# Moving one residual step and one set of feature combinations of a hybrid encoder block, and laying the FFN's buffers over dead ones

## The chip, the cores and the metric

The kernel runs on one core of a Trainium2 chip. A core has five engines that run side by side, each through its own queue in order: TensorE (matmuls and transposes; PE in the profile, PEld for its weight loads), VectorE (DVE), ScalarE (ACT), GpSimd (POOL) and SyncE (SP), which here issues nearly all DMA transfers. The metric is the device time of one execution in microseconds, lower is better.

## The reference

One layer of a residual block on 2048 tokens of width 1024, everything in float32:

```
h   = rms_norm(x);  proj = h @ w_in
yA  = chunk_band_attention(q, k, v, rel_bias)      # 8 heads, band of 9 chunks of 64
yB  = rwkv7_time_mix(...)                          # recurrent state over time
m   = sigmoid(gA) * (yA @ proj_a) + sigmoid(gB) * (yB @ proj_b)
x   = x + rms_norm(m @ w_out)
u   = square(relu(rms_norm(x) @ w_up)) @ w_down    # 1024 -> 4096 -> 1024
x   = x + rms_norm(u)
```

## The kernel before

The 2048 tokens are cut into four groups of 512 (g = 0 to 3). Every float32 matmul operand is split into a rounded part and a remainder (`split`, lines 69 and 70: ScalarE casts the high part, VectorE subtracts it), and a product is made of three matmuls (`mm3`, line 78).

*Mixing.* For each group: the recurrent part, attention, then `phase_merge`. The merge first computes eight branches of A (`branch`, lines 927 to 932: load a gate block th from gd, load and split a block of proj_a, 12 matmuls into ps_p, then VectorE multiplies), adds the B branch mb that was stored to md (line 948), and splits the sum into mh and ml. Then it runs the w_out loop (line 958): two halves n of eight blocks k, each block 4 x 3 matmuls into ps_o. After each half ScalarE copies ps_o to o (line 964), and o is stored to od (line 1229).

*Work laid beside.* `after` is a generator of steps that the merge calls between its w_out blocks in the second half and empties at its end. In the first three groups it prepares the next group's features. From group 1 on it runs `residuals(g - 1)`: for each of four tiles of 128 tokens it loads o and x, normalises (ACT lines 980 and 987, POOL lines 94 to 99, VectorE lines 982 to 989), stores x1, transposes xn on TensorE (ps_ht, line 994, 8 transposes per tile) and stores the result to ht (line 997). In group 3 it first runs `combinations(0)`, which reads the stored features ht of groups 0 and 1 and writes four differences of feature blocks to td (lines 1018 to 1025). They are the operands of the FFN's up stage, which saves one of eight block products by Strassen's scheme (in Winograd's form).

*FFN.* Two halves of two groups each: `phase_up` and `phase_down`. `first_half` loads and splits bl and bh (lines 1031 to 1039), the features of the half's first group. `phase_up` makes in its first eight steps products that need only those (A11 B11, A12 B21), with the splits of the other operands T (t2, t3, t1, b22, t4, from td and ht, line 1069) between them; then come 16 steps with the rest. The hidden values go to DRAM (ad, line 1094). `phase_down` has 16 steps (fg) of 96 matmuls into ps_dn (line 78), whose results VectorE adds into u (lines 1170 and 1172); its operands fop are loaded and split one step at a time. After th = 1 of each step but the last it runs one step of `beside`: the residual of group 3 (four steps), `combinations(1)` (four), `first_half(2)` (four). In the last step `final` normalises, adds x1 and stores the result (lines 1178 to 1193).

*Order and memory.* The program's order is that of the Python calls as a priority; the tile framework places instructions of each engine, and may put later work ahead where it is ready. SBUF is handed out by pools as two stacks, one from the left and one from the right. When a pool closes, its bytes go to the next pool, and a tile there waits until the tiles that were in those bytes are done (`reuse_waits="tile"`). So the places of the pools settle what a load or a split must wait for.

Before the change, in the FFN the left stack has z (32 KB per partition), b (32 KB) and raw (16 KB), then in the up stage the weight operands ops (28 KB) and the T operands (80 KB), and in the down stage ring (32 KB) and ffo; the right stack has cb, then up or the sums u.

Of the kernel before, what the change touches and what calls it, by code (L numbers as in the profile page):

```python
# [49 lines left out]
class Block:  # L50
# [883 lines left out]

    def phase_merge(self, g, o, between):

        tc, nc, a = self.tc, self.nc, self.a
        with ExitStack() as ctx:
# [70 lines left out]
    def combinations(self, half, mp):  # L1009


        nc = self.nc
        KH = KB // 2
        g0, g1 = (self.ht[2 * half + i] for i in range(2))
        for k in range(KH):
            b = mp.tile([P, 4, G], F32, tag="cmb", bufs=1, name="cmb")
            for i, src in enumerate((g0[:, k], g1[:, k], g0[:, KH + k], g1[:, KH + k])):
                nc.sync.dma_start(b[:, i], src)
            t = mp.tile([P, 4, G], F32, tag="cmt", bufs=1, name="cmt")
            for o, x, y in (  # L1020
                (t[:, 0], b[:, 1], b[:, 0]), (t[:, 2], b[:, 3], b[:, 1]),
                (t[:, 1], b[:, 3], t[:, 0]), (t[:, 3], b[:, 2], t[:, 1]),
            ):
                nc.vector.tensor_tensor(o, x, y, ALU.subtract)
            nc.sync.dma_start(self.td[half][:, :, k], t)
            yield
# [7 lines left out]
    def first_half(self, g, bp):  # L1034

        bh, bl = (bp.tile([P, KB, G], F32R, tag="b" + x, name="b" + x) for x in "hl")
        for k in range(0, KB, 2):
# [3 lines left out]
            yield  # L1041
        self.b1 = bh, bl

    def phase_up(self, half, zp, rp, cb, pn, early):
# [6 lines left out]
        with ExitStack() as ctx:  # L1051
            e = ctx.enter_context
            sp = e(tc.tile_pool(name="ops", bufs=1, reuse_waits="tile"))
            tb = e(tc.tile_pool(name="ht", bufs=1, reuse_waits="tile"))
# [4 lines left out]
            T = {}  # L1059

            def operands():
                td, g1 = self.td[half], self.ht[2 * half + 1]
                for n, src in (
                    ("t2", td[:, 1]), ("t3", td[:, 2]), ("t1", td[:, 0]), ("b22", g1[:, hi4]), ("t4", td[:, 3])
                ):
                    h, l = T[n] = [tb.tile([P, KH, G], F32R, name=n + x) for x in "hl"]
                    for k in (0, 2):
# [69 lines left out]
    def phase_down(self, half, zp, rp, cb, pn, beside_of):  # L1137
# [4 lines left out]
        with ExitStack() as ctx:  # L1142
            e = ctx.enter_context
            ring = e(tc.tile_pool(name="ring", bufs=2, reuse_waits="tile"))
            op = e(tc.tile_pool(name="ffo", bufs=2, reuse_waits="tile"))
            pt = e(tc.tile_pool(name="ffp", bufs=2, space=PSUM, reuse_waits="tile"))
            cp = e(tc.tile_pool(name="ffu", bufs=1, side="right", reuse_waits="tile"))
            u = [cp.tile([P, D], F32, name=f"u{t}") for t in range(NT)]
            beside = beside_of(op, pt)

# [44 lines left out]
            for fg in range(NF // 2):  # L1195
                ws = [load(2 * fg), load(2 * fg + 1)]
                last = fg == NF // 2 - 1
                if last:
                    gt = self.gain(op, a["post_ffn_g"], "g_post2", 2)
                for th in range(2):  # L1200
                    down(th, ws, fg == 0)
                    if last:
                        final(th)
                    elif th:
                        advance(beside, 1)


    def run(self):
        tc, e = self.tc, None
        with ExitStack() as ctx, ExitStack() as mixing:  # L1210
# [10 lines left out]
            for g in range(self.NG):  # L1221
                self.phase_rwkv(g)
                self.phase_attention(g)
                with tc.tile_pool(name="p0", bufs=2, reuse_waits="tile") as sp, \
                     tc.tile_pool(name="p0p", bufs=2, space=PSUM, reuse_waits="tile") as pt:
                    o = [sp.tile([P, D], F32, tag="o", bufs=GT, name=f"o{t}") for t in range(GT)]
                    self.phase_merge(g, o, self.after(g, sp, pt))
                    for t in range(GT):
                        self.nc.sync.dma_start(self.od[g][t], o[t])
# [56 lines left out]
```

## Time and profile before

| | us |
|---|---|
| median of 3 runs | 3496.29 |
| lowest and highest of them | 3493.8, 3499.4 |
| the profiled execution | 3489.82 |
| span of its profile | 3488.1 |

In the profile, a row of the engines' summary gives busy time, its share of the span and the number of instructions. A row of the timeline gives the start, the length, the engine, the line of the kernel, the operation, the tile written and the tiles read, the shape and the count; in brackets stands how long the engine was idle before it, and what released it. A line such as L69 or L78 is that of a helper, so the tile's name tells which stage it is from. The stages follow one another in the span so: the four mixing groups up to 2113 us, the first up stage up to 2454, the first down stage up to 2807, the second up stage up to 3119, the second down stage up to the end.

### The profile page before, as it was taken

What the parts mean: (1) busy time and instruction counts of PE and PEld (TensorE: products, weight loads), DVE (VectorE), ACT (ScalarE), POOL (GpSimd) and SP (SyncE); (2) the same over time, 40 slices, a digit from 0 to 9 for tenths busy, and PEclk for the clock granted to TensorE, in tenths of its full rate; (3) what the DMA queues carried; (4) which work ended last, traced back from release to release, by engine and by line L of the source; (5) the groups of instructions that cost most, each with busy time, mean ns of one, the idle gap of its engine ahead of it and who ended that gap; (6) DMA issues with size and microseconds to landing.
All of it is one profiled execution on the core that took longest, in us unless ns stands there. A gap on an engine that the chain in (4) does not pass through costs nothing. (4 is left out here: it accounts for less than half of the span.)

```text
span 3488.1 us, 50851 instructions
## 1 busy us (share of the span) xinstructions
PE 3312.6 (95%) x19233; PEld 2679.4 (77%) x19233; DVE 2425.0 (70%) x4206; ACT 1430.4 (41%) x2399; POOL 353.4 (10%) x700
## 2 busy tenths in 40 slices
PE   7999999999998999999999986999999989999998
PEld 5777777777876777877777875888888878888886
DVE  5774756756756766856775865777876687776667
ACT  4434644436644436635445635333311143331112
POOL 2210002100012110002110000111100021100001
PEclk9999999999999999999999998999999999999999
DMA  5223453125364125365224279434753274343333
GB/s 148 79 86 124 137 180 116 60 91 179 128 224 148 59 86 183 111 226 163 65 92 143 88 243 301 134 121 137 246 190 97 87 241 140 109 156 97 97 97 109
DMA packets 430125, 481.15 MB, mean 138 GB/s; under 512 B 19564, under 2 KB 322864, under 8 KB 429880
## 3 DMA queue, kind: packets, MB, share of 16 engines
q1 hardware_dynamic: 419640, 444.34, 39.9%
q0 software_dynamic: 10240, 33.56, 2.5%
q8 instruction: 151, 2.47, 0.3%
q14 instruction: 94, 0.77, 0.1%
HBM read 356.16 MB, written 124.81 MB: 138 GB/s over the span
## 5 line engine op out<-in xcount | busy, mean ns | idle before, releaser
L78 PE MATMUL ps_dn<-fop 128*128 128x512 f32 x3072 | 698.3, 389 | 1.7 <-DVE u L1172 1.7
L78 PEld LDWEIGHTS ps_dn<-fop 128*128 128x128 f32 x3072 | 576.1, 188 | 122.0 <-DVE u L1172 2.6
L78 PE MATMUL psd<-hh,whi 128*128 128x512 f32 x1344 | 546.8, 407 | 17.1 <-ACT whi L69 14.0
L78 PE MATMUL psd<-hl,whi 128*128 128x512 f32 x1344 | 543.8, 405 | 0.0
L78 PE MATMUL psd<-hh,wlo 128*128 128x512 f32 x1344 | 540.6, 402 | 0.7 <-DVE wlo L70 0.5
L69 ACT CAST whi<-wraw 128x1024 fp32r<-128x1024 f32 (+1 forms) x296 | 255.7, 864 | 582.3 <-PE psd L78 391.6
L70 DVE TENSOR_TENSOR wlo<-wraw,whi 128x1024 fp32r<-128x1024 f32 (+1 forms) x296 | 292.6, 989 | 257.7 <-ACT whi L69 193.5
L1172 DVE TENSOR_TENSOR u<-u,ps_dn 128x512 f32<-128x512 f32 x480 | 323.5, 685 | 175.3 <-PE ps_dn L78 174.6
L78 PEld LDWEIGHTS psd<-hh,whi 128*128 128x128 f32 x1344 | 257.8, 192 | 71.5 <-ACT whi L69 15.7
L78 PEld LDWEIGHTS psd<-hh,wlo 128*128 128x128 f32 x1344 | 257.6, 192 | 52.8 <-DVE wlo L70 3.6
L78 PEld LDWEIGHTS psd<-hl,whi 128*128 128x128 f32 x1344 | 258.3, 192 | 48.5
L69 ACT CAST fop<-wdraw 128x1024 fp32r<-128x1024 f32 x64 | 67.3, 1051 | 469.8 <-DVE u L1172 321.5
L78 PE MATMUL ps_p<-yh,whi 128*128 128x512 f32 x256 | 107.3, 419 | 23.8 <-DVE th L932 23.4
L1094 POOL DMA_DIRECT2D ad<-r x128 | 69.6, 544 | 573.2 <-DVE r L1093 556.6
L69 ACT CAST s12h<-s 128x1024 fp32r<-128x1024 f32 x32 | 33.6, 1051 | 185.8 <-PE ps_u L78 185.8
L826 DVE CUSTOM_DVE_ANT_0 sc<-bias,ps_s 128x640 f32<-128x640 f32 (+4 forms) x128 | 93.3, 729 | 21.9 <-PE ps_pt L838 12.9
L958 PE MATMUL ps_o<-wlo,mh 128*128 128x512 f32 x256 | 102.3, 400 | 5.1 <-DVE wlo L70 4.9
L831 ACT ACTIVATE sc<-sc,mn 128x640 f32<-128x640 f32 (+4 forms) x128 | 97.8, 764 | 22.3 <-DVE mn L826 21.5
L78 PE MATMUL ps_p<-yh,wlo 128*128 128x512 f32 x256 | 105.3, 411 | 0.0
L78 PE MATMUL ps_p<-yl,whi 128*128 128x512 f32 x256 | 104.9, 410 | 0.0
L843 DVE TENSOR_TENSOR PTl<-ps_pt,PTh 128x640 fp32r<-128x640 f32 (+4 forms) x128 | 94.2, 736 | 12.9 <-ACT PTh L842 12.1
L958 PE MATMUL ps_o<-whi,mh 128*128 128x512 f32 x256 | 100.2, 399 | 3.0 <-ACT whi L69 3.0
(346 smaller groups left out, 6578.1 us busy)
## 6 DMA issues: line engine op xcount, KB each, us to landing
wraw<-in_w_in_dram SPq DMA_DIRECT2D x168, 512.0 KB
wraw<-in_w_up_dram SPq DMA_DIRECT2D x80, 512.0 KB
ad<-r POOLq DMA_DIRECT2D x128, 256.0 KB, 2.7
wdraw<-in_w_down_dram SPq DMA_DIRECT2D x64, 512.0 KB
araw<-ad SPq DMA_DIRECT2D x64, 512.0 KB
gd<-gate SPq DMA_DIRECT2D x64, 256.0 KB
th<-gd SPq DMA_DIRECT2D x64, 256.0 KB
wraw<-in_w_out_dram SPq DMA_DIRECT2D x64, 256.0 KB
```

Source lines behind the costliest of these rows:

```text
L69: self.nc.scalar.copy(hi, src)
L70: self.nc.vector.tensor_tensor(lo, src, hi.bitcast(F32), ALU.subtract)
L78: mm = nc.tensor.matmul(ps, l, r, start=n == 0, stop=n == last).ins
L826: nc.vector.tensor_tensor_reduce(sc[:, 0:n], bias[:, s0:640], pss[:, c0 : c0 + n], 1.0, 3.0e38, ALU.add, ALU.min, mn,)
L831: nc.scalar.activation(sc[:, 0:n], sc[:, 0:n], AF.Exp, scale=-1.0, bias=mn, accum_out=sm)
L843: nc.vector.tensor_tensor(lv, pst[:, 0:nk], hv.bitcast(F32), ALU.subtract)
L958: nc.tensor.matmul(ps[t], l[:, k, ts], r[:, 0], start=k == 0 and j == 0, stop=k == KB - 1 and j == 2)
L1094: nc.gpsimd.dma_start(self.ad[fb][:, th], r)
L1172: nc.vector.tensor_tensor(u[t][:, ns], u[t][:, ns], ps, ALU.add)
```

## The change

Five things are done.

1. `residuals(2)` is no longer run in the merge of group 3. It runs beside the first down stage, ahead of `residuals(3)`; that stage now has 16 beside steps instead of 12, two of them in its first step fg = 0.
2. `combinations(0)` is no longer run between the w_out blocks of group 3 but beside the branches, one step after each second branch. Its tiles cmb come from a pool p1 of their own, opened ahead of p0, with two buffers. So nothing is left in `after` for group 3.
3. `combinations` works in place: the four differences are written over the loaded blocks, in another order, and the tile cmt is gone. The number of subtractions and transfers is the same. The operand loads take the blocks of td by their new places.
4. `first_half` sets `self.b1` ahead of its first step, and the T operands are allocated at the start of `phase_up` in the order t4, b22, t2, t3, t1 (loaded in the old order).
5. Pools change sides and order. Right stack now: raw and cb; in the down stage then ffb (the beside work's tiles, a new pool), ring and ffo. Left stack: z, b; in the up stage then T, up and ops; in the down stage u. The gain of the last normalisation has one buffer instead of two.

```
     def after(self, g, sp, pt):
         if g + 1 < self.NG:
             yield from self.phase_norm(g + 1, sp, pt)
-        if g == 3:
-            yield from self.combinations(0, sp)
-        if g > 0:
+        if 0 < g < 3:
             yield from self.residuals(g - 1, sp, pt)
...
@@ phase_merge, the branches
                 self.split(mh[:, i], ml[:, i], t)
+                advance(early, i % 2)
...
@@ combinations
-            b = mp.tile([P, 4, G], F32, tag="cmb", bufs=1, name="cmb")
+            b = mp.tile([P, 4, G], F32, tag="cmb", bufs=bufs, name="cmb")
...
-            t = mp.tile([P, 4, G], F32, tag="cmt", bufs=1, name="cmt")
-            for o, x, y in (
-                (t[:, 0], b[:, 1], b[:, 0]), (t[:, 2], b[:, 3], b[:, 1]),
-                (t[:, 1], b[:, 3], t[:, 0]), (t[:, 3], b[:, 2], t[:, 1]),
-            ):
-                nc.vector.tensor_tensor(o, x, y, ALU.subtract)
-            nc.sync.dma_start(self.td[half][:, :, k], t)
+            for o, x, y in ((0, 1, 0), (1, 3, 1), (3, 3, 0), (2, 2, 3)):
+                nc.vector.tensor_tensor(b[:, o], b[:, x], b[:, y], ALU.subtract)
+            nc.sync.dma_start(self.td[half][:, :, k], b)
...
@@ phase_up
-            sp = e(tc.tile_pool(name="ops", bufs=1, reuse_waits="tile"))
             tb = e(tc.tile_pool(name="ht", bufs=1, reuse_waits="tile"))
-            up = e(tc.tile_pool(name="up", bufs=1, side="right", reuse_waits="tile"))
+            up = e(tc.tile_pool(name="up", bufs=1, reuse_waits="tile"))
+            sp = e(tc.tile_pool(name="ops", bufs=1, reuse_waits="tile"))
...
@@ phase_down
-            ring = e(tc.tile_pool(name="ring", bufs=2, reuse_waits="tile"))
-            op = e(tc.tile_pool(name="ffo", bufs=2, reuse_waits="tile"))
+            cp = e(tc.tile_pool(name="ffu", bufs=1, reuse_waits="tile"))
+            bp = e(tc.tile_pool(name="ffb", bufs=2, side="right", reuse_waits="tile"))
+            ring = e(tc.tile_pool(name="ring", bufs=2, side="right", reuse_waits="tile"))
+            op = e(tc.tile_pool(name="ffo", bufs=2, side="right", reuse_waits="tile"))
...
-                    elif th:
+                    elif th or fg == 0:
                         advance(beside, 1)
+            advance(beside)
...
@@ run
-                with tc.tile_pool(name="p0", bufs=2, reuse_waits="tile") as sp, \
-                     tc.tile_pool(name="p0p", bufs=2, space=PSUM, reuse_waits="tile") as pt:
+                with ExitStack() as c:
+                    early = iter(())
+                    if g == self.NG - 1:
+                        early = self.combinations(0, c.enter_context(tc.tile_pool(name="p1", bufs=1, reuse_waits="tile")), 2)
...
-            rp = e(tc.tile_pool(name="raw", bufs=4, reuse_waits="tile"))
+            rp = e(tc.tile_pool(name="raw", bufs=4, side="right", reuse_waits="tile"))
...
             def beside(op, pt):
-                yield from self.residuals(self.NG - 1, op, pt, 1)
+                for g in (2, 3):
+                    yield from self.residuals(g, op, pt, 1)
                 yield from self.combinations(1, op)
                 yield from self.first_half(2, bp)
```

More of the change, by code (lines that the diff above doesn't have):

```diff
@@ L933, in branch, with phase_merge @@
         return t
-    def phase_merge(self, g, o, between):
+    def phase_merge(self, g, o, between, early=iter(())):
         tc, nc, a = self.tc, self.nc, self.a
@@ L1003, in after, with combinations @@
             yield from self.phase_norm(g + 1, sp, pt)
-        if g == 3:
-            yield from self.combinations(0, sp)
-        if g > 0:
+        if 0 < g < 3:
             yield from self.residuals(g - 1, sp, pt)
-    def combinations(self, half, mp):
+    def combinations(self, half, mp, bufs=1):
         nc = self.nc
@@ L1034, in first_half @@
     def first_half(self, g, bp):
-        bh, bl = (bp.tile([P, KB, G], F32R, tag="b" + x, name="b" + x) for x in "hl")
+        bh, bl = self.b1 = [bp.tile([P, KB, G], F32R, tag="b" + x, name="b" + x) for x in "hl"]
         for k in range(0, KB, 2):
@@ L1041, in first_half @@
             yield
-        self.b1 = bh, bl
     def phase_up(self, half, zp, rp, cb, pn, early):
@@ L1058, in phase_up @@
             z = zp.tile([P, early, G], F32, tag="z", name="z")
-            T = {}
+            T = {
+                n: [tb.tile([P, KH, G], F32R, name=n + x) for x in "hl"] for n in ("t4", "b22", "t2", "t3", "t1")
+            }
             def operands():
@@ L1063, in operands @@
                 for n, src in (
-                    ("t2", td[:, 1]), ("t3", td[:, 2]), ("t1", td[:, 0]), ("b22", g1[:, hi4]), ("t4", td[:, 3])
+                    ("t2", td[:, 3]), ("t3", td[:, 1]), ("t1", td[:, 0]), ("b22", g1[:, hi4]), ("t4", td[:, 2])
                 ):
-                    h, l = T[n] = [tb.tile([P, KH, G], F32R, name=n + x) for x in "hl"]
+                    h, l = T[n]
                     for k in (0, 2):
@@ L1143, in phase_down @@
             e = ctx.enter_context
[L1144 to L1145 removed]
+            cp = e(tc.tile_pool(name="ffu", bufs=1, reuse_waits="tile"))
+            bp = e(tc.tile_pool(name="ffb", bufs=2, side="right", reuse_waits="tile"))
+            ring = e(tc.tile_pool(name="ring", bufs=2, side="right", reuse_waits="tile"))
+            op = e(tc.tile_pool(name="ffo", bufs=2, side="right", reuse_waits="tile"))
             pt = e(tc.tile_pool(name="ffp", bufs=2, space=PSUM, reuse_waits="tile"))
[L1147 removed]
             u = [cp.tile([P, D], F32, name=f"u{t}") for t in range(NT)]
[L1149 removed]
+            beside = beside_of(bp, pt)
             def load(fb):
@@ L1198, in phase_down @@
                 if last:
-                    gt = self.gain(op, a["post_ffn_g"], "g_post2", 2)
+                    gt = self.gain(op, a["post_ffn_g"], "g_post2")
                 for th in range(2):
@@ L1223, in run @@
                 self.phase_attention(g)
-                with tc.tile_pool(name="p0", bufs=2, reuse_waits="tile") as sp, \
-                     tc.tile_pool(name="p0p", bufs=2, space=PSUM, reuse_waits="tile") as pt:
+                with ExitStack() as c:
+                    early = iter(())
+                    if g == self.NG - 1:
+                        early = self.combinations(0, c.enter_context(tc.tile_pool(name="p1", bufs=1, reuse_waits="tile")), 2)
+                    sp = c.enter_context(tc.tile_pool(name="p0", bufs=2, reuse_waits="tile"))
+                    pt = c.enter_context(tc.tile_pool(name="p0p", bufs=2, space=PSUM, reuse_waits="tile"))
                     o = [sp.tile([P, D], F32, tag="o", bufs=GT, name=f"o{t}") for t in range(GT)]
-                    self.phase_merge(g, o, self.after(g, sp, pt))
+                    self.phase_merge(g, o, self.after(g, sp, pt), early)
                     for t in range(GT):
```

2 lines of the change are left out of this document (1 added, 1 removed).

## The prediction

> **What bounds the kernel now.** I read the page's busy shares first, to find the engine that sets the time.
>
> ```profile
> PE 3312.6 (95%) x19233; PEld 2679.4 (77%) x19233; DVE 2425.0 (70%) x4206; ACT 1430.4 (41%) x2399; POOL 353.4 (10%) x700
> PEclk9999999999999999999999998999999999999999
> ```
>
> TensorE is busy 95% of the span and its clock falls in only one slice, number 25 of 40, which begins at 24 x 87.2 = 2093 us. That is where the last merge ends and the FFN begins. So the time is TensorE's own work plus the stretches where it stands, and a change that removes no matmul can gain only in those stretches. The second view is the busy time in stretches around this place (columns: stretch, length, then each engine's busy time and instruction count, granted clock, DMA share, GB/s).
>
> ```profile
> 2021.00:2060.90 39.90, 33.03 (x128) 25.59 (x127) 24.72 (x39) 10.45 (x19) 0.00 (x0) 0.91 0.80 262
> 2061.00:2113.30 52.30, 46.65 (x195) 36.85 (x194) 27.66 (x38) 18.75 (x32) 3.50 (x10) 0.97 0.84 286
> ...
> 2112.90:2144.90 32.00, 6.38 (x34) 4.91 (x32) 12.49 (x10) 15.04 (x23) 4.45 (x10) 0.61 0.86 292
> ...
> 2150.00:2160.00 10.00, 10.00 (x45) 8.22 (x44) 8.13 (x9) 7.40 (x9) 0.79 (x1) 0.97 1.10 351
> ...
> 2200.00:2225.00 25.00, 25.00 (x112) 20.71 (x111) 21.20 (x31) 8.85 (x12) 3.25 (x6) 1.00 0.35 110
> ```
>
> The last row is TensorE at its steady pace: 25 us for 112 matmuls, 0.2232 us each. By that pace the branches (2021 to 2060.9, 128 matmuls, 28.6 us) lose 11.3 us, the w_out loop (192 matmuls, 42.9 us, in 52.3) loses 9.4 us, and between 2112.9 and 2144.9 almost all is lost. The third view is the order in time across that last hole.
>
> ```profile
> 2112.93 0.40 PE L958 MATMUL ps_o<-whi,ml 128*128 128x512 f32 x1
> ...
> 2123.32 1.97 PE L994 MATMUL ps_ht<-ident,xn 128*128 128x128 f32 x8 [7.69 <-DVE xn L989]
> ...
> 2133.54 1.95 SPq L1039 DMA_DIRECT2D bl<-ht  x4
> ...
> 2138.23 1.04 ACT L1031 CAST bh<-bl 128x1024 fp32r<-128x1024 f32 x1 [5.18 <-DMA bl<-ht]
> ...
> 2143.86 1.04 ACT L69 CAST a1h<-wraw 128x1024 fp32r<-128x1024 f32 x1 [0.72 <-DMA wraw<-in_w_up_dram]
> ...
> 2144.96 0.79 PE L78 MATMUL ps_u<-bh,a1h 128*128 128x512 f32 x1 [12.57 <-ACT a1h L69]
> ```
>
> After the last w_out matmul at 2112.93 the residual of the third group still runs, tile by tile, with TensorE doing only its transposes; only then does SP load the first feature halves (2133.54), and the first FFN product starts at 2144.96.
>
> **The change, part by part.**
>
> (1) *The hole before the FFN.* The residual of group 2 leaves this place, and the FFN's buffers are laid where the mixing's dead ones were, so the four loads of bl, the first w_up blocks and their splits no longer need the last merge to be over. What the hole is worth:
>
> ```profile
> 2144.90:2150.00 5.10, 5.00 (x11) 3.55 (x12) 0.00 (x0) 0.00 (x0) 0.50 1.11 351
> ```
>
> These are the instructions of ps_u alone: 12 products (by the weight loads; matmul records can be missing) by 2150, at clock 0.50. At the steady pace they take 2.7 us and could follow the last w_out matmul at 2113.16. So 2150.0 - 2113.16 - 2.7 = **34.1 us** if the seam closes. Ends: 34.1, and 20.0 if the loads of bl stay behind the merge in SP's queue (they would be issued at about 2113.5 instead of 2133.54, everything behind them unchanged). I take **31**, near the upper end: bl and bh lie over the features h and one buffer of the combinations, raw over constants of the mixing, a1 over attention tiles, all dead by 2061, 50 us before they are needed. What is then late next is the ten operand splits; they have eight early steps of 24 matmuls, 43 us, as before.
>
> (2) *The residual beside the first down stage.* It adds 4 tiles with 8 transposes each. The nearest rows are those of group 3, which is already there:
>
> ```profile
> 2498.30 1.03 PE L994 MATMUL ps_ht<-ident,xn 128*128 128x128 f32 x8
> 2499.09 22.03 PE L78 MATMUL ps_dn<-fop 128*128 128x512 f32 x96
> ...
> 2453.60:2475.00 21.40, 21.40 (x96) 17.70 (x96) 19.50 (x25) 8.37 (x12) 5.00 (x11) 1.00 0.73 258
> ...
> 2563.00:2585.00 22.00, 22.00 (x99) 18.22 (x98) 19.60 (x29) 3.90 (x4) 0.00 (x0) 1.00 0.72 249
> ...
> 2700.00:2722.00 22.00, 22.00 (x99) 18.22 (x98) 15.27 (x21) 4.14 (x5) 0.00 (x0) 1.00 0.33 98
> ```
>
> Eight transposes hold TensorE 2499.09 - 2498.30 = 0.79 us, four tiles 3.2 us. VectorE: 15.3 us in 22 without anything beside it, 19.5 with one residual tile in the first step. Only the first step now gets two, 19.5 + 4.2 = 23.7 against 21.4, at worst 2.3 us. The down stage ran full with 19.6, so I take **-3.2**; ends -3.2 and -5.5. The loads, the stores of x1 and ht and SP's two gains per group (DMA share 0.30 to 0.73 here) are hidden by those 22 us steps; without that cover the wait would show as PSUM evictions late on VectorE. The second combinations and the second first_half move four steps later, still a step ahead of the stage's end, and with one buffer instead of two tiles each turn waits for its store; at one turn per 22 us this costs nothing.
>
> (3) *From the first down stage to the second up stage.* Not what the change names, but the new layout reaches it:
>
> ```profile
> 2801.20 5.74 PE L78 MATMUL ps_dn<-fop 128*128 128x512 f32 x24 [0.86 <-DVE u L1172]
> ...
> 2807.05 1.03 ACT L69 CAST a1h<-wraw 128x1024 fp32r<-128x1024 f32 x1
> ...
> 2808.13 0.50 PE L78 MATMUL ps_u<-bh,a1h 128*128 128x512 f32 x1 [1.19 <-ACT a1h L69]
> ...
> 2814.01 1.22 DVE L70 TENSOR_TENSOR a1l<-wraw,a1h 128x1024 fp32r<-128x1024 f32 x1
> ...
> 2815.28 0.79 PE L78 MATMUL ps_u<-bh,a1l 128*128 128x512 f32 x1 [5.94 <-DVE a1l L70]
> ...
> 2819.89 0.39 PE L78 MATMUL ps_u<-bh,a1h 128*128 128x512 f32 x1
> ```
>
> The split of the first w_up block starts at 2807.05, right after the last ps_dn: its raw block was there, so it waited for memory, since the up operands lie over the down stage's ring. Its second half then stands on VectorE behind the final normalisation. In the new layout (left: z, b, u; right: raw, cb, ffb, ring, ffo) a1, s12 and s3 fall on ffb, dead after the combinations, so they can be split some steps earlier. Worth: 15 products run between 2806.8 and 2819.89; 13.1 - 15 x 0.2232 = 9.7 us. Late next is VectorE, which still has the final work. I take **8**; ends 0 (if a1 still meets a live tile) and 9.7.
>
> (4) *Combinations and residual out of the w_out loop.* Of its 9.4 lost us these waits carry most:
>
> ```profile
> 2041.73 0.77 PE L78 MATMUL ps_p<-yh,whi 128*128 128x512 f32 x1 [4.17 <-DVE th L932]
> ...
> 2075.88 0.50 PE L958 MATMUL ps_o<-whi,mh 128*128 128x512 f32 x1 [1.17 <-ACT whi L69]
> 2078.67 0.64 PE L958 MATMUL ps_o<-wlo,mh 128*128 128x512 f32 x1 [2.29 <-DVE wlo L70]
> 2095.32 0.50 PE L958 MATMUL ps_o<-wlo,mh 128*128 128x512 f32 x1 [1.18 <-DVE wlo L70]
> ...
> 2075.47 1.28 DVE L982 SCALAR_TENSOR_TENSOR o_prev<-o_prev,rs_p,g_post 128x1024 f32<-128x1024 f32 x1 [3.94 <-POOL rs_p L99]
> ```
>
> VectorE stood 3.94 us for the residual's rs_p with the w_out split wlo behind it. That goes. In its place come the four bl splits and the first w_up splits, which also can hold ACT for a DMA. Ends 0 and 9.4; I take **6**.
>
> (5) *Combinations in the branches.* The same 16 subtracts and the same bytes, in place:
>
> ```profile
> L1024 DVE TENSOR_TENSOR cmt<-cmb x16: 683/686/693, 2028.1 to 2597.0; 128x512 f32<-128x512 f32 x16
> ...
> 2021.38 0.43 SPq L1018 DMA_DIRECT2D cmb<-ht  x1
> ...
> 2039.95 0.53 SPq L1025 DMA_DIRECT2D td<-cmt  x1
> ...
> 2090.76 1.21 SPq L1018 DMA_DIRECT2D cmb<-ht  x1
> ...
> 2104.33 0.53 SPq L1025 DMA_DIRECT2D td<-cmt  x1
> ```
>
> Four turns of 4 x 0.685 = 2.7 us VectorE, in a stretch where it is busy 24.7 of 39.9. The first turn already runs in the branches (2021.38 to 2040.5), though written later, so only three move. The branches already wait for late data (2041.73, 4.17 us); more traffic can add, two buffers and no residual loads can take away. Ends -16 (by bytes, next part) and +11 (nothing lost any more); I take **0**.
>
> Sum: 31 - 3.2 + 8 + 6 + 0 = 41.8 us. The profiled execution took 3489.8 us (span 3488.1), the median of the three shown is 3496.3, 0.19% more; I take the gain off the median: **3454.5 us**.
>
> **The rivals.**
>
> *Branches bound by the DMA engines.* Eight branches load 3 x 256 KB each, 6.3 MB; the combinations load and store 8.4 MB. 14.7 MB at the 262 GB/s of that stretch are 56 us, 16 more than the 39.9; at the 351 GB/s seen from 2150 to 2160 they are 42. For: share 0.80 already. Against: the first turn can start earlier and the last can trail into w_out. With 14 us lost: 3468.5. The Trainium skill, DMA: Bandwidth & Descriptors, Specifications, gives an HBM limit of about 358 GB/s for a core; by it 14.7 MB take at least 41 us, an estimate, so the stage would be just full. The row with 351 agrees.
>
> *The loads of bl stay behind the merge* (the change does only half of what its layout is for): (1) gives 20.0, so 3465.5. For: SP's queue goes in order, and the stores of o and the w_out loads stand in it. Against: the first cmb load at 2021.38 shows that transfers are already issued long ahead of their place in the program.
>
> *a1 still meets live memory* at the second up stage: (3) gives 0, 3462.5.
>
> *Slower: SP's queue is held by the combinations.* A load of turn k+2 waits for the store of turn k, and the th, mb and w loads of the next branches stand behind it. If the four turns go one after the other at 18.6 us each (the first turn, from its first load to the issue of its store), the branches take 74.4 instead of 39.9, 34.5 lost; the same queue keeps the FFN loads late (20.0 in (1)) and w_out gains nothing: 20 + 8 - 3.2 - 34.5 = -9.7, 3506. It turns to slower only from turns of (39.9 + 24.8) / 4 = 16.2 us. Against: the last turn took 13.6 us with one buffer, and two buffers let turns overlap.
>
> **How the numbers follow.** Chances: forecast 0.57, DMA-bound branches 0.17, bl behind the merge 0.14, a1 on live memory 0.08, slower 0.04. Without the slower case all gain more than 0.2% (7 us, about what a measurement of this kernel can tell from no change): faster 0.95, within 0.01, slower 0.04. The forecast by itself reaches from 3443 (about 11 us more, if (1), (3) and (4) come to their upper ends and the branches gain some) to 3462. The range reaches on to the two main rivals: 3443 to 3470.
>
> **What would show it.** Right: no ps_ht between the last ps_o and the first ps_u, that seam under 3 us at full clock; bl loads issued before the last ps_o; 64 transposes instead of 32 in the first down stage with no ps_dn wait beside them; a1l before the last ps_dn at the second seam; w_out's 192 matmuls in some 46 us. Wrong: branches longer than 45 us with th waiting for DMA, a seam of 10 us or more that ACT's bh ends, or ps_dn waiting for VectorE's u in the first steps.

## The result and the profile after

| | before | after |
|---|---|---|
| median, us | 3495.33 (6 runs, 3489.81 to 3499.4) | 3461.93 (6 runs, 3459.0 to 3469.01) |
| ratio to before | | 0.9907, 95% interval 0.9895 to 0.992 |
| span of the profiled execution, us | 3488.1 | 3460.6 |

The change saves 33.4 us by the medians and 27.5 us by the two profiled spans. The profiled execution of before was one of the fastest of its six; the accounts below are made of profiled executions, so they add up to 27.5.

The summary of the engines after, the rows that answer to the first two of before:

```profile
PE 3310.7 (96%) x19233; PEld 2677.4 (77%) x19233; DVE 2421.3 (70%) x4206; ACT 1429.6 (41%) x2399; POOL 352.7 (10%) x700
PEclk9999999999999999999999999999999999999999
```

As many instructions as before, 1.9 us less of busy TensorE, and slice 25 of the clock is a 9 now. The gain is time in which TensorE stood.

To see where it went, I cut both executions at the starts of six products of TensorE: the last product of attention, the first and the last ps_o of group 3, the first product with t2h (the end of the eight early up steps), the first ps_dn, and the first t2h product of the second half. The passage from one stage to the next is called a seam here; it is counted together with the early up steps, so that what it pushes behind it is in the same number. "Merge" below is branches and w_out loop together.

| stretch, us | before | after | gain |
|---|---|---|---|
| up to the merge of group 3 | 2020.6 | 2020.8 | -0.2 |
| branches (attention to first ps_o) | 40.3 | 53.8 | **-13.5** |
| w_out loop | 52.0 | 48.2 | +3.8 |
| seam and early up steps | 79.7 | 44.9 | **+34.8** |
| rest of the first up stage | 261.3 | 261.3 | 0 |
| first down stage, second seam, early up steps | 407.3 | 404.0 | +3.3 |
| the rest | | | -0.7 |

The timeline of TensorE after, at the first seam and at the second one (start, length, engine, line, operation, shapes, count, idle time before it and what ended it):

```profile
2123.01 0.39 PE L78 MATMUL ps_u<-bh,a1h 128*128 128x512 f32 x1
...
2447.14 1.09 PE L995 MATMUL ps_ht<-ident,xn 128*128 128x128 f32 x8 [0.35 <-DVE xn L990]
2447.99 10.97 PE L78 MATMUL ps_dn<-fop 128*128 128x512 f32 x47
2459.05 1.09 PE L995 MATMUL ps_ht<-ident,xn 128*128 128x128 f32 x8
2459.90 2.32 PE L78 MATMUL ps_dn<-fop 128*128 128x512 f32 x9
...
2781.22 5.63 PE L78 MATMUL ps_dn<-fop 128*128 128x512 f32 x24
...
2786.69 0.39 PE L78 MATMUL ps_u<-bh,a1l 128*128 128x512 f32 x1
...
2794.56 0.50 PE L78 MATMUL ps_u<-bh,s12h 128*128 128x512 f32 x1 [0.68 <-ACT z L1096]
...
2818.16 0.50 PE L78 MATMUL ps_u<-bh,s3h 128*128 128x512 f32 x1 [1.29 <-DVE r L1087]
```

The first ps_u starts at 2123.01, at full clock and without a bracket: the first seam is closed. The moved transposes stand among ps_dn rows with one wait of 0.35 us. At the second seam no product waits for a1 any more, since its split had been made long before, as the rows of ScalarE and VectorE show:

```profile
2748.12 1.05 ACT L69 CAST a1h<-wraw 128x1024 fp32r<-128x1024 f32 x1 [2.76 <-DMA wraw<-in_w_up_dram]
...
2750.91 1.22 DVE L70 TENSOR_TENSOR a1l<-wraw,a1h 128x1024 fp32r<-128x1024 f32 x1
```

What is late there instead are the first evictions (z, 0.68 us, and r, 1.29 us).

The loss is in the branches. First the busy time in stretches after (stretch, length, busy time and count of each engine, granted clock, DMA share, GB/s): the branches, the first and the second half of the w_out loop, then ten microseconds inside the branches.

```profile
2021.00:2074.60 53.60, 35.71 (x129) 26.25 (x127) 32.61 (x51) 11.24 (x19) 0.00 (x0) 0.87 0.87 285
2074.60:2098.00 23.40, 21.94 (x88) 17.08 (x89) 14.58 (x18) 11.68 (x15) 0.00 (x0) 0.93 0.95 293
2098.00:2122.80 24.80, 23.90 (x106) 19.44 (x105) 6.76 (x9) 8.90 (x16) 0.00 (x0) 1.00 0.47 138
...
2060.00:2070.00 10.00, 6.30 (x18) 4.95 (x19) 6.01 (x10) 1.85 (x3) 0.00 (x0) 0.66 0.88 276
```

The DMA engines are busiest until 2098 (0.87 and 0.95 of the time) and half idle after it (0.47). In the branches TensorE is idle for 53.60 - 35.71 = 17.9 us (before: 6.9), and its 28.6 us of products take 35.7 (before: 33.0), as the granted clock is lower after each stop: in the last row 18 products take 6.30 us, 0.35 each instead of 0.22. So of the longer branches some 11.0 us are waits and 2.7 are slow products. The waits themselves, and SP's queue ahead of them:

```profile
2048.93 0.80 PE L78 MATMUL ps_p<-yh,whi 128*128 128x512 f32 x1 [6.09 <-ACT whi L69]
...
2063.70 0.79 PE L78 MATMUL ps_p<-yh,whi 128*128 128x512 f32 x1 [5.62 <-ACT whi L69]
...
2074.58 1.46 PE L959 MATMUL ps_o<-whi,mh 128*128 128x512 f32 x4 [2.85 <-ACT whi L69]
```

```profile
2042.16 0.91 SPq L1017 DMA_DIRECT2D cmb<-ht  x2
2043.11 0.43 SPq L62 DMA_DIRECT2D wraw<-in_proj_a_dram  x1
...
2051.52 3.61 SPq L1017 DMA_DIRECT2D cmb<-ht  x3
...
2058.50 0.43 SPq L62 DMA_DIRECT2D wraw<-in_proj_a_dram  x1
...
2064.29 3.70 SPq L1017 DMA_DIRECT2D cmb<-ht  x4
2068.09 0.94 SPq L62 DMA_DIRECT2D wraw<-in_w_out_dram  x2
```

All three waits end with whi, the rounded part of a weight block, and each such block (wraw) was issued right behind or soon after cmb loads of 256 KB each. The block issued at 2043.11 is cast at 2048.27, 5.2 us later. It is the fifth of the eight, and it was issued 22.3 us after the last product of attention; before, the fifth went out 12.5 us after it:

```profile
2033.10 0.38 SPq L62 DMA_DIRECT2D wraw<-in_proj_a_dram  x1
```

While TensorE stood in the two longest waits, the DMA engines of the kernel after weren't full:

```profile
2043.00:2049.00 6.00, 0.07 (x1) 0.07 (x1) 4.27 (x8) 1.75 (x3) 0.00 (x0) 0.92 0.78 257
2058.00:2064.00 6.00, 0.38 (x2) 0.30 (x2) 5.05 (x9) 1.24 (x2) 0.00 (x0) 0.80 0.72 220
```

Three causes were set against each other: the blocks stand behind cmb in SP's in-order queue (theory S); the DMA engines have too many bytes to move, wherever the loads are issued (theory B); or VectorE, busy with the 16 subtractions, hands back buffers late (theory V).

### The profile page after: what moved, and what is told of

It reads as the page before. It is cut to its first block, busy times and chain, and to the rows that moved or that the text cites. A ratio compares the mean times of both kernels' runs of the same rounds, so it can differ in the third digit from the quotient of the medians.

```text
span 3460.6 us, 50793 instructions
## 1 busy us (share of the span) xinstructions
PE 3310.7 (96%) x19233; PEld 2677.4 (77%) x19233; DVE 2421.3 (70%) x4206; ACT 1429.6 (41%) x2399; POOL 352.7 (10%) x700
## 5 line engine op out<-in xcount | busy, mean ns | idle before, releaser
L78 PE MATMUL psd<-hh,whi 128*128 128x512 f32 x1344 | 546.4, 407 | 16.7 <-ACT whi L69 13.5
L78 PEld LDWEIGHTS psd<-hh,whi 128*128 128x128 f32 x1344 | 258.3, 192 | 71.7 <-ACT whi L69 15.5
L78 PEld LDWEIGHTS psd<-hh,wlo 128*128 128x128 f32 x1344 | 258.0, 192 | 52.5 <-DVE wlo L70 3.5
L959 PE MATMUL ps_o<-wlo,mh 128*128 128x512 f32 x256 | 102.1, 399 | 1.1 <-DVE wlo L70 1.1
```

The lines of the kernel that those rows point to most:

```text
L78: mm = nc.tensor.matmul(ps, l, r, start=n == 0, stop=n == last).ins
L959: nc.tensor.matmul(ps[t], l[:, k, ts], r[:, 0], start=k == 0 and j == 0, stop=k == KB - 1 and j == 2)
```

## The experiments

All runs are set against the kernel before on the same chip. The stretch ahead of the merge ended between 2017.6 and 2029.8 us in the profiled executions of these kernels, though its code is the same in nearly all of them; so a difference of a few us is read from the stage and not from the total.

| run | median us | ratio, 95% interval | branches | w_out | merge | seam + early |
|---|---|---|---|---|---|---|
| after | 3461.93 | 0.9907 [0.9895, 0.992] | 53.8 | 48.2 | 102.0 | 44.9 |
| 1 combinations beside w_out | **3449.39** | 0.9879 [0.9865, 0.9894] | 39.2 | 48.3 | 87.5 | 44.9 |
| 2 combinations on POOL's queue | 3454.02 | 0.9895 [0.9877, 0.9914] | 40.1 | 53.9 | 94.0 | 44.9 |
| 3 four cmb buffers | 3461.63 | 0.9915 [0.99, 0.993] | 52.9 | 49.0 | 101.9 | 44.9 |
| 4 no subtractions | 3464.16 (one run) | | 55.3 | 47.2 | 102.5 | 44.9 |
| 5 branch weights on POOL's queue | 3464.82 | 0.9917 [0.9902, 0.9932] | 52.6 | 49.5 | 102.1 | 44.9 |
| 6 residual moved alone | 3479.18 | 0.9959 [0.9945, 0.9974] | 38.1 | 46.2 | 84.3 | 66.0 |
| 7 residual back in the merge | 3478.46 | 0.9957 [0.9942, 0.9972] | 52.5 | 55.7 | 108.2 | 52.3 |
| 8 as 1, on POOL's queue | 3458.75 | 0.9899 [0.9883, 0.9916] | 40.8 | 54.2 | 95.0 | 44.9 |
| 9 combinations between the loops | 3463.55 | 0.9926 [0.9908, 0.9944] | 48.5 | 54.6 | 103.1 | 44.9 |
| 10 all weights on POOL's queue | 3462.75 | 0.9921 [0.9905, 0.9936] | 44.8 | 54.4 | 99.2 | 44.9 |
| 11 half the bytes of the cmb loads | 3460.45 | 0.9903 [0.9886, 0.9919] | 42.9 | 50.1 | 93.0 | 44.9 |

**1. The combinations beside w_out again**, all else of the change kept.

```
-                    self.phase_merge(g, o, self.after(g, sp, pt), early)
+                    self.phase_merge(g, o, early if g == self.NG - 1 else self.after(g, sp, pt))
```

> The changed kernel with one thing undone: the first combinations run between the w_out blocks again, with their two buffers. In the changed kernel the branches (from 2021 us to the first ps_o) took 53.6 us against 39.9 before, the w_out loop 48.6 against 52.3. All theories have the branches back at 39 to 43 us. If the traffic is what costs (bytes), the loss moves into w_out: 56 to 60 us there, total time within 3 us of the changed kernel. If the place beside the branches is what costs (queue order or VectorE order), w_out takes 48 to 53 us and the time falls by 7 to 13 us, to about 3452.

Measured: 3449.39 us (3448.28 to 3451.89), faster than both kernels. The windows of the branches and of the w_out loop, and its cmb loads on SP:

```profile
2022.70:2061.90 39.20, 33.66 (x131) 26.09 (x130) 25.31 (x40) 10.46 (x19) 0.00 (x0) 0.91 0.84 267
2061.90:2110.20 48.30, 45.30 (x193) 35.22 (x192) 28.09 (x38) 20.74 (x31) 0.00 (x0) 1.00 0.92 292
```

```profile
2051.51 0.42 SPq L1017 DMA_DIRECT2D cmb<-ht  x1
...
2054.80 0.42 SPq L1017 DMA_DIRECT2D cmb<-ht  x1
...
2058.91 0.42 SPq L1017 DMA_DIRECT2D cmb<-ht  x1
```

The branches are back at 39.2 us, and the w_out loop is no longer than after. Nine of the 16 cmb loads still go out ahead of the first ps_o. These three stand one at a time among w_out's first weight blocks; the last seven follow as a pair, a three and a pair. The DMA engines are at 0.92 over the whole w_out loop, against 0.71 after. By length times rate the merge moves 10.5 + 14.1 = 24.6 MB; after it was 53.8 x 0.284 + 48.2 x 0.214 = 25.6 MB. So the total of the bytes does not set the merge's length, and the whole loss of the branches comes from the place of the combinations.

**2. Combinations beside the branches, issued by POOL** (the lines of `combinations(0)` alone).

```
-                nc.sync.dma_start(b[:, i], src)
+                (nc.sync if half else nc.gpsimd).dma_start(b[:, i], src)
...
-            nc.sync.dma_start(self.td[half][:, :, k], b)
+            (nc.sync if half else nc.gpsimd).dma_start(self.td[half][:, :, k], b)
```

> The changed kernel with the first combinations' 16 loads and 4 stores issued from GpSimd's queue instead of SP's; same bytes, same buffers, same subtracts. Theory S (loads of the branches stand in SP's queue behind cmb loads that wait for a buffer): branches 39 to 45 us, time lower by 8 to 13 us. Rival B (the DMA engines are full): branches stay at 51 to 55 us, no change of time. Rival V (subtracts that wait for cmb hold th on VectorE): also 51 to 55 us.

Measured: 3454.02 us (3450.23 to 3458.74); branches 40.1, but w_out 53.9. It speaks for S in the branches; it isn't clean, for the other queue also moved the transfers in time: eight of the 16 cmb loads went out ahead of the last product of attention, and only 40.1 x 0.280 = 11.2 MB fall into the branches, against 15.3 after. Also, twelve products of the last branch ran behind the first ps_o (as in run 8), so the last product of the branches ended 43.6 us after the last one of attention, and some 3 us of the 53.9 are the branches'.

**3. Four buffers of cmb instead of two.**

```
-                        early = self.combinations(0, c.enter_context(tc.tile_pool(name="p1", bufs=1, reuse_waits="tile")), 2)
+                        early = self.combinations(0, c.enter_context(tc.tile_pool(name="p1", bufs=1, reuse_waits="tile")), 4)
```

> The changed kernel with four cmb buffers instead of two: no cmb load ever waits for a store, the order in SP's queue is the same. Theory S, if the buffer wait at the queue's head is what holds the branch loads: branches 42 to 48 us, time lower by 5 to 11 us. S, if only the order of the queue counts: 51 to 54 us. Rival B: all loads come earlier and crowd the branches, 53 to 58 us. Rival V: 51 to 54 us, unless the subtracts' data come earlier.

Measured: 3461.63 us (3461.3 to 3463.74), branches 52.9: nothing. The waits of cmb loads for a free buffer are not the cause.

**4. Without the 16 subtractions of the first combinations** (the blocks are stored as they were loaded).

```
-            for o, x, y in ((0, 1, 0), (1, 3, 1), (3, 3, 0), (2, 2, 3)):
+            for o, x, y in ((0, 1, 0), (1, 3, 1), (3, 3, 0), (2, 2, 3)) if half else ():
```

> The changed kernel without the 16 subtractions of the first combinations (left out; the blocks are stored as loaded), so that VectorE has nothing to wait for there. Theory S and rival B: branches 50 to 54 us, since SP's queue and the bytes stay (a store can go a little earlier). Rival V: branches back at 40 to 44 us.

Measured: 3464.16 us, one run, branches 55.3. With 11 us less work on VectorE the branches are no shorter, as far as one run tells: V falls.

**5. Only the weights of group 3's A branches issued by POOL**, combinations and all the rest on SP.

```
-        nc.sync.dma_start(raw, src)
+        (q or nc.sync).dma_start(raw, src)
...
-        wh, wl = self.wsplit(w.rearrange("(k p) n -> p k n", p=P), "w", NP, P)
+        wh, wl = self.wsplit(w.rearrange("(k p) n -> p k n", p=P), "w", NP, P, q=self.nc.gpsimd if self.last and br == 0 else None)
...
+                self.last = g == self.NG - 1
```

> The changed kernel with the eight proj_a loads of the last group's branches issued from GpSimd's queue; the combinations' loads stay in SP's queue, beside the branches. Mirror of the run that moved the combinations' transfers. Theory S (what costs is that the branch weights stand in SP's queue behind th, mb and cmb loads): last ps_pv to last ps_o falls from 102.0 us to 90 to 95, time lower by 7 to 12 us. If instead it were only the number of transfers or their bytes: 100 to 103 us, no change.

Measured: 3464.82 us (3461.46 to 3466.55), no gain: a miss for S. The last product of the branches comes early, at 2061.89, but then TensorE, SP and ScalarE show this:

```profile
2071.55 1.65 PE L959 MATMUL ps_o<-whi,mh 128*128 128x512 f32 x3 [9.26 <-ACT whi L69]
```

```profile
2062.93 0.62 SPq L1017 DMA_DIRECT2D cmb<-ht  x1
2063.72 2.51 SPq L62 DMA_DIRECT2D wraw<-in_w_out_dram  x2
```

```profile
2070.88 1.36 ACT L69 CAST whi<-wraw 128x512 fp32r<-128x512 f32 x2 [2.55 <-DMA wraw<-in_w_out_dram]
```

What was won went into one wait of 9.26 us for the first w_out block, issued at 2063.72 behind cmb and cast 7 us later. That block was still in SP's queue, so the miss doesn't refute S for the branches: their last product ended 43.3 us after the last one of attention, against 50.9 after, and none of their waits ended with whi. 52.6 x 0.295 = 15.5 MB were moved up to there, as many as after.

**6. The kernel before with `residuals(2)` moved alone**: no new layout, combinations where they were.

```
-        if g > 0:
+        if 0 < g < 3:
...
-                    elif th:
+                    elif th or fg == 0:
...
-                yield from self.residuals(self.NG - 1, op, pt, 1)
+                for g in (2, 3):
+                    yield from self.residuals(g, op, pt, 1)
```

> The kernel before with one part alone: residuals(2) moved beside the first down stage (two steps in fg = 0), old places of the pools, combinations between the w_out blocks as before. Theory: merge like before or a little shorter in w_out (last ps_pv to last ps_o 87 to 92 us against 92.3), the seam before the FFN still open because bl lies over the o tiles that are stored at the merge's end: 10 to 14 us without ps_u, at half clock at its end, so 18 to 24 us gained there; -3.5 us for the transposes; the seam before the second up stage unchanged. Sum 15 to 25 us faster than before. Rival: the residual alone brings all of the first seam, 30 us or more.

Measured: 3479.18 us (3477.88 to 3480.73); by the ratio 14 us faster than before, just under what was expected. The merge is the shortest of all, 84.3 us, since the residual's bytes left it too, but the seam stays open:

```profile
2129.23 0.79 PE L78 MATMUL ps_u<-bh,a1h 128*128 128x512 f32 x1 [17.52 <-ACT a1h L69]
```

TensorE stands 17.52 us for the first w_up block. SP issued bl only at 2117.38, when it had waited for a store of o (od<-o), and w_up behind it: the memory was not free earlier.

**7. The changed kernel with `residuals(2)` back at the end of the merge**: new layout and early combinations, residual as before.

```
-        if 0 < g < 3:
+        if g > 0:
...
-                for g in (2, 3):
-                    yield from self.residuals(g, op, pt, 1)
+                yield from self.residuals(3, op, pt, 1)
```

> The changed kernel with only the residual of group 2 put back at the end of the merge; places of the pools and combinations as in the changed kernel. Theory: ps_u can start while the residual runs, since bl, raw and a1 no longer wait for the merge, so the first seam costs little more than the residual's transposes (0.8 us each) and its share of VectorE and ACT: 3 to 10 us without ps_u; the first down stage is 3.6 us shorter; total within 8 us of the changed kernel. Rival: the residual itself holds the seam, by its order on ACT, VectorE and SP: 20 us or more of it come back.

Measured: 3478.46 us (3476.0 to 3480.81), 16.5 us above after, a miss. By stages: merge +6.2, seam +7.4, first down stage and second seam -4.7; the stretch ahead of the merge was 9.0 us longer in this execution. The seam's own wait is small,

```profile
2140.75 0.50 PE L78 MATMUL ps_u<-bh,a1h 128*128 128x512 f32 x1 [2.40 <-ACT a1h L69]
```

so the layout with the early combinations takes 79.7 - 52.3 = 27.4 of the seam's 34.8 us, and moving the residual alone 79.7 - 66.0 = 13.7: they overlap, and both are needed for 44.9.

**8. As 1, with the combinations issued by POOL** (the edits of 1 and 2 together).

```
-                nc.sync.dma_start(b[:, i], src)
+                (nc.sync if half else nc.gpsimd).dma_start(b[:, i], src)
...
-                    self.phase_merge(g, o, self.after(g, sp, pt), early)
+                    self.phase_merge(g, o, early if g == self.NG - 1 else self.after(g, sp, pt))
```

> The changed kernel with the combinations between the w_out blocks again and their transfers on GpSimd's queue: both remedies together. Theory S: the branches keep their 39 us and w_out loses nothing to SP's queue, 84 to 88 us from last ps_pv to last ps_o (87.5 with the first remedy alone), time 3445 to 3452. Rival: GpSimd's issues come at other times and crowd the branches, 90 us or more.

Measured: 3458.75 us (3457.29 to 3459.74), merge 95.0: a miss, slower than 1, although SP's queue is free of the combinations. POOL, SP, VectorE and a window of this run:

```profile
2045.79 2.25 POOL L1017 DMA_DIRECT2D cmb<-ht  x4
```

```profile
2048.02 0.32 SPq L927 DMA_DIRECT2D th<-gd  x1
```

```profile
2055.35 0.69 DVE L932 SCALAR_TENSOR_TENSOR th<-th,ps_p 128x512 f32<-128x512 f32 x1 [5.38 <-DMA th<-gd]
```

```profile
2040.00:2050.00 10.00, 6.03 (x26) 4.29 (x25) 6.27 (x10) 2.48 (x4) 2.89 (x5) 1.00 1.02 359
```

POOL issues four loads, 1 MB, in a burst; th, 256 KB, is issued on the other queue at its end, and VectorE gets it 7.3 us later, with the DMA engines full (share 1.02, 359 GB/s). An own queue did not help this load, which came behind a burst in the same engines. Theory S in its plain form, the order on SP alone, can't explain this wait; what remains of it is an order of all loads, on the queues or in the engines. The next expectations call that the order theory, and theory B for the whole merge the byte theory.

**9. The four turns written between the branch loop and the w_out loop.**

```
-                advance(early, i % 2)
             self.yctx.close()
+            advance(early)
```

> The changed kernel with the four turns of the first combinations written between the branch loop and the w_out loop: behind all branches, ahead of all w_out blocks. Order theory (what costs is that loads of a turn stand ahead of the next branch's loads): the branches return to 39 to 42 us, from 53.8; the w_out loop keeps the turns ahead of its own weight loads and takes 50 to 56, against 48.2; merge 90 to 96, total 3449 to 3456. Byte theory (the stage of 102 us is as long as its bytes and matmuls make it): merge 100 to 104 as in the changed kernel, total 3460 to 3464. If the turns cost nothing ahead of w_out because that loop needs only 256 KB a block: merge 87 to 89, total as in the kernel with the turns beside w_out, 3449.

Measured: 3463.55 us (3461.31 to 3466.78), branches 48.5 and w_out 54.6. Some of the cmb loads are still placed in the branches, ahead of their place in the program, and the rest stand ahead of the w_out blocks:

```profile
2019.50:2068.00 48.50, 33.92 (x130) 25.73 (x128) 30.38 (x48) 11.66 (x20) 0.00 (x0) 0.88 0.85 272
2068.00:2098.00 30.00, 25.35 (x84) 19.06 (x85) 17.20 (x22) 11.39 (x14) 0.00 (x0) 0.79 0.95 301
2098.00:2122.60 24.60, 24.60 (x109) 20.17 (x108) 5.93 (x9) 8.58 (x15) 0.00 (x0) 1.00 0.45 137
```

The order theory's 39 to 42 for the branches is missed only because the wait for the first w_out block, 8.2 us, lies ahead of the first ps_o: the last product of the branches ended at 40.3. Its 90 to 96 for the merge is missed by 7, and the merge is as long as after. Again the engines are busiest first and half idle in the last 25 us, where TensorE runs without a gap.

**10. All weights of group 3's merge issued by POOL**: the edit of 5 and, for the w_out blocks,

```
-                    wh, wl = self.wsplit(a["w_out"][k * P : (k + 1) * P, None, n * 512 : (n + 1) * 512], "w", 1, 512)
+                    wh, wl = self.wsplit(a["w_out"][k * P : (k + 1) * P, None, n * 512 : (n + 1) * 512], "w", 1, 512, q=nc.gpsimd if self.last else None)
```

> The changed kernel, combinations beside the branches on SP, but the weight blocks of the last group's A branches and of its w_out loop issued from POOL. Order theory, SP's queue as its place: no weight waits behind cmb, th or mb any more; the 9.26 us wait of the first w_out block in the kernel with only the branch weights on POOL goes, so branches 41 to 44 and w_out 46 to 49, merge 88 to 93, total 3449 to 3456. Order theory, the DMA engines as its place: the bursts of cmb still fill the engines ahead of the weights, merge 98 to 103, total 3458 to 3464. Byte theory: merge 100 to 104, total 3460 to 3464.

Measured: 3462.75 us (3459.67 to 3464.83), merge 99.2. That is in the span expected with the DMA engines as the place, not SP's queue: no weight waits behind cmb there, and yet

```profile
2065.50:2098.00 32.50, 26.32 (x100) 19.13 (x99) 18.24 (x25) 12.29 (x18) 4.04 (x8) 0.95 1.08 345
2098.00:2119.90 21.90, 21.63 (x95) 17.25 (x94) 7.12 (x9) 8.26 (x14) 2.95 (x6) 1.00 0.24 80
```

in the first part of the w_out loop TensorE is idle for 6.2 us with the engines at 1.08 and 345 GB/s, and the last 21.9 us use only 80 GB/s. The Trainium skill says as much in DMA: Bandwidth & Descriptors, Issuing engines are not separate DMA queues: transfers run on the same 16 engines and interleave, whichever engine started them, and a second issuer saves only the time of issuing. Runs 5 and 10 agree, with 102.1 and 99.2 us of merge against 102.0 after, and so does 8, with 95.0 against 87.5 in 1. The 94.0 of run 2 came with loads that were issued earlier.

**11. Half the bytes, as many loads.** Its engine theory is theory B for the branches alone: not the merge's bytes count, but those that fall into the branches. The first combinations read only the left 256 tokens of each block and use them for both halves, so the right half of their input is left out.

```
-                nc.sync.dma_start(b[:, i], src)
+                    nc.sync.dma_start(b[:, i, : G // 2], src[:, : G // 2])
...
+                    for c in (G // 2, 0):
+                        nc.vector.tensor_tensor(b[:, o, c : c + G // 2], b[:, x, : G // 2], b[:, y, : G // 2], ALU.subtract)
```

> The changed kernel, with the first combinations reading only the left 256 of the 512 tokens of each feature block and using them for both halves: as many loads on SP's queue (16), each of 128 KB instead of 256 KB, so 2.1 of some 25.6 MB of the merge less; the stores and VectorE's work stay (32 subtractions of half the width). Leaves out the right half of the combinations' input. Engine theory (the branches last as long as the bytes that are put into them take at 285 to 295 GB/s): 15.3 - 2.1 = 13.2 MB, branches 45 to 47 us against 53.8, total 3452 to 3456. Queue theory (the loads cost by their place and number on SP): branches 52 to 55, total 3460 to 3464.

The window of its branches:

```profile
2025.60:2068.50 42.90, 32.15 (x130) 24.91 (x129) 29.80 (x59) 10.63 (x18) 0.00 (x0) 0.88 0.84 274
```

Measured: branches 42.9, below even the 45 to 47 of the engine theory, against 52 to 55 of the queue theory. It isn't clean: 42.9 x 0.274 = 11.8 MB were moved in the branches, 3.5 less than after and not 2.1, so some loads also came later than in the changed kernel. The total, 3460.45 us (3458.64 to 3462.66), missed its 3452 to 3456: the merge is 9.0 us shorter than after, but the stretch ahead of it ended 4.8 us later in the profiled execution.

**What follows together.** That the combinations' place beside the branches costs the merge 14.5 us is shown by 1, which undoes this alone. V falls (4), buffers fall (3), and so does the merge's total of bytes (1). S and B for the branches are left, and these runs don't separate them.

| kernel | MB in the branches | GB/s | branches, us | last branch product ends, us |
|---|---|---|---|---|
| 6 | 9.9 | 259 | 38.1 | 38.2 |
| before | 10.4 | 259 | 40.3 | 40.4 |
| 1 | 10.5 | 267 | 39.2 | 39.3 |
| 2 | 11.2 | 280 | 40.1 | 43.6 |
| 8 | 11.6 | 285 | 40.8 | 44.8 |
| 11 | 11.8 | 274 | 42.9 | 43.1 |
| 10 | 12.6 | 282 | 44.8 | 44.9 |
| 9 | 13.2 | 272 | 48.5 | 40.3 |
| 3 | 15.1 | 286 | 52.9 | 50.8 |
| 4 | 15.2 | 274 | 55.3 | 55.5 |
| after | 15.3 | 284 | 53.8 | 50.9 |
| 7 | 15.4 | 293 | 52.5 | 50.7 |
| 5 | 15.5 | 295 | 52.6 | 43.3 |

Bytes are length times rate of the window; the last column counts from the last product of attention. For B: the rate stays within 259 to 295 GB/s while the bytes grow by half, and 11, with fewer bytes in as many loads, takes 9.0 us off the merge. But such a table could also run the other way (a longer stage moves more), and the engines were at only 0.78 and 0.72 in the two longest waits of the kernel after. For S: with the branch weights out of SP's queue and the same loads to make (5, 10), no wait for whi is left in the branches, and their last product ends 7.6 and 6.0 us earlier than after, with nearly all cmb loads issued by then. But the merge hardly gains, since TensorE then waits in the w_out loop instead. The reading that fits all runs is that the combinations' bytes stand ahead of the loads that TensorE needs next, in SP's queue or in the engines, and that the order decides which of these loads is late. It is argued, not shown.

Open is also why the w_out loop takes 48.3 us in 1, with 14.1 MB in it, and 54 in 2, 8, 9 and 10, with 12.4 to 13.0. In 2 and 8 part of it is the branches' own products. For the rest the likeliest reason, argued and not tested alone, is the order within it: in 1 the first cmb loads stand singly between weight blocks, in the others bursts stand ahead of them.

## Why the prediction came out as it did

The forecast was 3454.5 us and the range 3443 to 3470; measured were 3461.93, inside, 7.4 above the forecast.

| step | taken | measured |
|---|---|---|
| (1) hole before the FFN | +31 | +34.8 |
| (2) residual in the first down stage | -3.2 | -4.7 |
| (3) first down to second up stage | +8 | +8.0 |
| (4) w_out loop | +6 | +3.8 |
| (5) combinations in the branches | 0 | **-13.5** |

(The sum of the measured ones is 28.4; with the rest, -0.7, and the -0.2 ahead of the merge it is the 27.5 of the spans. Run 7 parts (2) and (3): it has the new layout without the moved residual, and its stretch from the first ps_dn to the second half's t2h took 399.3 us, against 407.3 before and 404.0 after.)

(1) came to its upper end, 34.1, and 0.7 us past it. bl and the first w_up blocks were there in time; run 7 shows that the layout, with the combinations early, brings 27.4 us of it without the residual's move, and run 6 that this move brings 13.7 without the layout. The rival "bl behind the merge" did not come: its first load was issued 40 us before the first ps_u.

```profile
2082.24 0.67 SPq L1034 DMA_DIRECT2D bl<-ht  x1
```

(2) held: 4.7 lies between its ends of 3.2 and 5.5. The cover that it named, the 22 us steps, kept all but a wait of 0.35 us; its price of 0.79 us a tile was too low, for from the first to the last ps_dn TensorE was busy 4.0 us longer than in run 7, 1.0 a tile. (3) held for its reason: a1's split had moved from 2807 to 2748, before the last ps_dn, so the rival "a1 on live memory" fell. It came to 8.0 of at most 9.7 us; the two waits for z and r, ScalarE's and VectorE's evictions, are 2.0 together, and VectorE was named as late next.

(4) had the right sign and was too large by 2.2. Its working overrated the waits: the one of 4.17 us at 2041.73 is a branch's (ps_p), and the three of w_out come to 4.6, half of the 9.4 and not most of it. The other reason is in the first half of the loop after, which follows the 2.85 us wait at 2074.58: there the granted clock was 0.93, and two waits came, 1.30 us for a weight (whi) and 0.16 for wlo. With the residual moved alone (6), the combinations still in the loop, it took 46.2 us, a gain of 5.8.

**(5) is the step that failed.** It weighed more traffic against two buffers and no residual loads and took 0, between ends of -16 and +11. The traffic won: -13.5, nearly the 14 of the rival "branches bound by the DMA engines". That rival, given 0.17, had the place and the size, and the bytes: its working has 14.7 MB, and 15.3 were moved. That full engines are the mechanism is not shown, as said above; the queue's order, which the slower rival named, has a part in it. The DMA rival's argument against itself was wrong: it said that the first turn (four loads, four subtractions and a store) can start earlier and the last trail into w_out. The first turn did start as early as before (2021.55), but all 16 cmb loads went out ahead of the first ps_o, and only the last store, at 2077.38, trailed. The turns were written one after each second branch and so ahead of the next branch's loads. The engines had most room at the end of the w_out loop, at 138 GB/s.

The sign that was to show it wrong, branches longer than 45 us, came, but of TensorE's 17.9 idle us 14.6 were waits for weights (whi) and 1.7 for th, which was named.

The Trainium skill's figure that the rival cited (DMA: Bandwidth & Descriptors, Specifications, about 358 GB/s for a core) was a poor price: by it the stage would take at least 41 us, an estimate, while its mean rate was 284 GB/s and it took 53.8. Nor is it a ceiling here. This is run 1's rate in 40 equal slices of 2021 to 2122 us, 2.5 us each:

```profile
GB/s 105 294 192 309 312 251 279 260 309 359 272 313 259 281 161 261 291 368 378 211 268 282 248 350 216 402 208 329 299 263 260 267 339 298 277 309 415 338 273 368
```

Single slices reach 402 and 415, and the five us from 2123 of the same run have 419. The same page's Bandwidth section has up to 425 GB/s for one core whose partner is idle. Here the kernel runs on one core, and these figures agree with that. The mean of a stage with mixed transfers is what the sum needed, and that stands in the windows.

By the stages the sum is 28.4 where 41.8 was taken, 13.4 less, and (5) alone is 13.5. That the forecast was still only 7.4 off is luck in part. The rival's sum, 41.8 - 14 = 27.8 us, is close to the 27.5 of the two profiled executions; taken off the median it gave 3468.5, and measured were 3461.9. By the medians the gain is 33.4 us, since the profiled execution of before was at the lower end of its runs. So 5.9 us of unexplained difference between profile and median helped the forecast.

## What to carry to other kernels

When work is moved beside other work, count the bytes that the receiving stage will hold and divide by the rate which that stage already reaches (here 259 to 295 GB/s): the branches, at a DMA share of 0.80 before, took 13.5 us more for 4.9 MB more, though VectorE had room for the work. Look also at the issue times of the loads that the busiest engine needs next, and put prefetches behind them (one at a time is argued here, not tested alone); another queue did not get a small load past a burst. Where a seam stands open both for work that is left and for memory that isn't free, expect each cure alone to give only a part.

## What the runs showed of the hardware that was not expected

- A stop of TensorE costs more than its length: in the branches after, the granted clock was 0.66 in the stretch 2060 to 2070 and a product took 0.35 us there instead of 0.22; 2.7 of the 13.7 us lost against before are slow products. The Trainium skill, TensorE: Matmul & The Clock Gate, What's actually happening, gives half the clock after an idle window of some 3.4 us. The trace agrees: the waits of 6.09 and 5.62 us are longer than that, and behind them the clock was 0.50 from 2049 to 2052 and from 2064 to 2068.
- Loads issued in a row can hold the issuing engine: four cmb loads took SP 3.70 us at 2064.29, where the DMA share was 1.02 up to 2068, while single ones took 0.42 in run 1, and a burst of four on POOL took 2.25 in run 8. That the full engines are the reason is not shown.
- A core's DMA engines can have room while TensorE stands for a load: 257 and 220 GB/s in the two longest waits after, 419 in five us of run 1.
- The stretch ahead of the merge, 2020 us long, ended up to 9 us later from one kernel to the next, although nearly nothing was changed in it; what sets this was not looked into.
